# Strassen pairs of a feed-forward layer: another order of the weight splits, row sums spread over three columns, and 13 state units moved into the pairs

## Chip, cores and metric

The kernel runs on one core of one Trainium2 chip. The metric is the device time of one execution in microseconds (us). The kernel before takes 1158.74 us (median of 3 runs, 1157.66 to 1161.28).

## What is computed

One layer of a decoder: 512 prompt tokens and 8 sample tokens (520 columns), width 1024. A modulated norm, one input projection, a pooling branch and a state-space branch, a gated merge and an output projection make up the first 700 us; the change touches none of that. What it touches is the feed-forward block and one small state update:

```python
gt, up = jnp.split(h2 @ w_ffn_in, 2, axis=-1)      # 1024 -> 2 x 2816
x = x + g2 * ((jax.nn.silu(gt) * up) @ w_ffn_out)  # 2816 -> 1024
# sample tokens, one step of the recurrent state: h = h * decay + (dt x) B
```

Everything is float32. A matmul of float32 precision is made of three matmuls on split operands: `hi` is the operand rounded to the PE's format (a copy on ScalarE), `lo` the rest (a subtraction on VectorE), and the product is hi·hi + hi·lo + lo·hi.

## The kernel before

**Columns.** The 2816 hidden channels are 22 columns of 128. A plain column j (`ffn`) multiplies two weight tiles, gate `wg` and up `wu` (128 x 1024 each, 512 KB), with the activations `hh`/`hl` (8 k-tiles of 128 x 520): 8 k-steps for each, 3 matmuls, 2 halves of 260 tokens. Then `ffn_end` applies SiLU on ScalarE and the product on VectorE, into the row `as[j]`.

**Pairs.** Columns 3 to 19 without 8 and 14 (`WINO`, 15 of them) compute gate and up together by one level of Strassen's scheme in Winograd's form (`wino`): seven products of half size instead of eight, 7 x 12 = 84 matmuls of 260 columns. They are called pairs below, since gate and up go together. The scheme needs sums of the activation blocks (`tt`, made once by `sums_of_rows`, `row_cuts` and `more_row_cuts` in rows `as[10]` to `as[17]`) and sums of the weight blocks of each pair. Weights of pair j+1 are prepared while PE multiplies pair j:

- `wino_first(j+1)`: splits one block of u into wx (`wxeh`, `wxel`), starts two sums on POOL (lines 1514 and 1515), then applies SiLU (ScalarE, 1573) and the product (VectorE, 1572) left over from pair j-1, splits the whole gate tile into wg (`wghi`, `wglo`) and starts two more sums on POOL (1523 and 1524), which overwrite parts of it.
- `wino_second(j+1)`: splits the result into wz (`wzhi`, `wzlo`).
- `wino_third(j)`: splits the sums in u into wy (`wyuh`, `wyul`); these two have one buffer each, so that they are made in pair j itself, after the PE has read the ones of pair j-1.

PE's order in a pair is the products g (two), x, z, y, z, y, 12 matmuls each; results are drained by ScalarE (1560) and VectorE (1557), the last of them the addition of the second y product to f2.

**Order.** From `ffn_act` on the program order of PE, ScalarE, VectorE, POOL and the SP queue is the order in which the program states them: each engine works through its own list and waits at the first instruction that is not ready. All weight loads go through SP, and so do the loads of the states; the stores of the states go through POOL's queue.

**Loads.** `pair_load(j+2)` in pair j loads two 512 KB tiles. There are three buffers `raw`; the u tile of an odd pair has a buffer `ur` of its own. Near the plain columns 8 and 14 the next plain column's first tile (wg14, wg20) is loaded early and holds one of the three buffers until it is split.

**Output.** After columns 20 and 21, `ffn_out` makes 8 output columns of 22 k-steps (weights `wfo`, three tiles a column); the last two go together in `last_pair`.

**State units.** `sample_states` handles 32 units of the sample state. A unit loads 256 KB of state `h` and 128 KB of `bb` (a row copied to all partitions), multiplies h by the decay on POOL (1352), makes dt x B with four ScalarE instructions (1358), adds on VectorE (1359) and stores 256 KB from POOL's queue (1360). Unit n asks for the loads of unit n+2. Before, all 32 run inside output columns 0 to 5: five in each of columns 0 to 3, six in columns 4 and 5 (`STEPS`).

Of the kernel before, what the change touches and what calls it, by code (L numbers as in the profile page):

```python
# [16 lines left out]
P = 128  # L17
T = 520
TP = 512
# [24 lines left out]
WARM = 17  # L44
NFS = 3
NU = 40
WINO = [j for j in range(3, 20) if j not in (8, 14)]
STEPS = (4, 8, 12, 16, 20), (3, 6, 10, 13, 17, 20)

SLICES = ((0, 1), (1, 3), (3, 5), (5, 7), (7, 8))  # L50
U_SH1, U_SC1, U_G1, U_SH2, U_SC2, U_G2 = (8 * i for i in range(6))
# [3 lines left out]
def tile_decoder(ctx: ExitStack, tc: tile.TileContext, I: dict, O: dict):  # L55
# [23 lines left out]
    def opened(name, side=None):  # L79
        pool = tc.tile_pool(name=name, bufs=1, **({"side": side} if side else {}))  # L80
        return pool, pool.__enter__()
# [54 lines left out]
    def whole(ps):  # L136
        return [(ps[:, :, :H2], 0, T)]
# [1185 lines left out]
        G["al"] = []  # L1323

    states = {}

    def state_unit(n):

# [2 lines left out]
    def state_load(n):  # L1331
        if n >= 32:
            return
        g, b = state_unit(n)
        sp = G["hs"]
        h = sp.tile([P, 2, 2, P], F32, tag="hs", name=f"hs{n}", bufs=4)
        bb = sp.tile([P, 2, P], F32, tag="bb", name=f"bb{n}", bufs=3)
        nc.sync.dma_start(out=h, in_=I["sssm"][g, :, b : b + 2])
        nc.sync.dma_start(out=bb, in_=dbc[g, 0, b : b + 2].unsqueeze(0).broadcast_to([P, 2, P]))
        states[n] = h, bb  # L1340

    def sample_states():


        for n in range(2):
            state_load(n)
        for n in range(32):
            g, b = state_unit(n)
            state_load(n + 2)
            h, bb = states.pop(n)  # L1350
            at = dtx[:, 1, 2 * g : 2 * g + 2, b : b + 2].rearrange("p j b -> p b j")
            nc.gpsimd.tensor_tensor(h, h, at.unsqueeze(3).broadcast_to([P, 2, 2, P]), ALU.mult)  # L1352
            t = G["ff"].tile([P, T], F32, tag="fs", name=f"ht{n}", bufs=NFS)[:, 0:TP]
            t = t.rearrange("p (b j n) -> p b j n", b=2, j=2)
            for i in range(2):
                for j in range(2):
                    x = xds[:, 2 * g + j, b + i : b + i + 1]
                    nc.scalar.activation(t[:, i, j], bb[:, i], AF.Identity, bias=0.0, scale=x)  # L1358
            nc.vector.tensor_tensor(h, h, t, ALU.add)  # L1359
            nc.gpsimd.dma_start(out=O["ssms"][g, :, b : b + 2], in_=h)  # L1360
            yield True
# [36 lines left out]
    def out_rows_open():  # L1398
        left()
        closed(G["we_"])  # L1400
        closed(G["tt_"])
        G["hx_"], hx = opened("hx")
        G["ah"] = [hx.tile([P, T], F32R, name=f"ah{k}") for k in range(NF)]
        G["hs_"], G["hs"] = opened("hs")

    def out_row(k):

# [28 lines left out]
    def ffn(j):  # L1436
        def fn(wg, wu):
            xh, xl = (lambda k: G["hh"][:, k]), (lambda k: G["hl"][:, k])
            left()
            pg = column([wg], xh, xl)  # L1440
            if j + 1 in WINO:
                wino_first(j + 1)
                pair_load(j + 2)
            pu = column([wu], xh, xl)
            if j + 1 in WINO:
                wino_second(j + 1)
            ffn_end(j, whole(pg), whole(pu))

        return fn
# [12 lines left out]
            t = G["as"][10 + 4 * q + i].rearrange("p (k c) -> p k c", c=H2)  # L1462
            split(*(x[:, 2 * q : 2 * q + 2] for x in G["tt"][i]), t)

    def sums_of_rows():
        v, p = nc.vector.tensor_tensor, nc.gpsimd.tensor_tensor
        add, minus = ALU.add, ALU.subtract
        for q in range(2):
            ks = slice(2 * q, 2 * q + 2)
            b = [[[hblock(n, r, c)[:, ks].bitcast(F32) for c in range(2)] for r in range(2)] for n in ("hh", "hl")]  # L1470
            t1, t2, t3, t4 = (G["as"][10 + 4 * q + i].rearrange("p (k c) -> p k c", c=H2) for i in range(4))
            v(t1, b[0][0][1], b[0][0][0], minus)
            v(t1, t1, b[1][0][1], add)
            v(t1, t1, b[1][0][0], minus)
            v(t2, b[0][1][1], t1, minus)
            v(t2, t2, b[1][1][1], add)
            p(t4, b[0][1][0], t2, minus)
            p(t4, t4, b[1][1][0], add)
            p(t3, b[0][1][1], b[0][0][1], minus)
            p(t3, t3, b[1][1][1], add)  # L1480
            p(t3, t3, b[1][0][1], minus)
        for q in range(2):
            row_cuts(q, 0, 1)

    def more_row_cuts():
        for q in range(2):
            row_cuts(q, 3, 2)

    WW = {}

# [14 lines left out]
    def wino_first(n, mult=None, silu=None):  # L1505


        if n in WINO:
            g, u = WW["raw", n]
            a11, a12, a21, a22 = g[:, 0:4], g[:, 4:8], u[:, 0:4], u[:, 4:8]  # L1510
            WW["x", n] = [G["we"].tile([P, 4, P], F32R, tag=t, name=f"wx{t}{n}", bufs=2) for t in ("eh", "el")]
            split(*WW["x", n], a22)
            v = nc.gpsimd.tensor_tensor
            v(a22, a21, a22, ALU.add)
            v(a21, a11, a21, ALU.subtract)
        elif n <= WINO[-1]:
            ahead(len(W["made"]) + 1)
        if silu:
            silu()
            mult()  # L1520
        if n in WINO:
            split(*wide(n, "g"), g)
            v(a11, a22, a11, ALU.subtract)  # L1523
            v(a12, a12, a11, ALU.subtract)  # L1524

    def wino_second(n):

        if n in WINO:
            split(*wide(n, "z"), WW["raw", n][0])
        else:  # L1530
            ahead(len(W["made"]) + 1, 1)
# [6 lines left out]
    def wino(j):  # L1538
        def fn():
            f1, f2 = (G["ff"].tile([P, T], F32, tag="fs", name=f"fs{j}_{i}", bufs=NFS) for i in range(2))  # L1540
            u2, u4 = f1[:, 0:H2], f2[:, H2:T]
            s = G["as"][j]
            sa, sb = s[:, 0:H2], s[:, H2:T]
            tt = G["tt"]
            B = lambda r, c: (hblock("hh", r, c), hblock("hl", r, c))
            twice = lambda ap: ap.unsqueeze(1).broadcast_to([P, 2, H2])

            def mult(kind, half, x, o=None):
                hi, lo = WW[kind, j]
                o = bank()[:, 0:H2] if o is None else o  # L1550
                for k in range(4):
                    q = 4 * half + k
                    for a, b, f, e in ((hi, x[0], k == 0, False), (hi, x[1], False, False), (lo, x[0], False, k == 3)):
                        nc.tensor.matmul(o, a[:, q], b[:, k], start=f, stop=e)  # L1554
                return o

            add = lambda out, a, b: nc.vector.tensor_tensor(out, a, b, ALU.add)
            m = main()
            wino_first(j + 1, *G.pop("left", ()))
            nc.scalar.copy(u2, mult("g", 0, B(0, 0)))  # L1560
            add(sa, mult("g", 1, B(1, 0)), u2)
            wino_third(j)
            pair_load(j + 2)
            mult("x", 0, tt[3], m[:, 0, 0:H2])
            add(u2, mult("z", 0, tt[1]), u2)
            mult("y", 1, tt[0], m[:, 1, 0:H2])
            wino_second(j + 1)
            add(halves(f2), m[:, :, 0:H2], twice(u2))
            add(sb, mult("z", 1, B(1, 1)), u4)
            add(halves(f2), twice(mult("y", 0, tt[2])), halves(f2))  # L1570
            G["left"] = (
                lambda: nc.vector.tensor_tensor(s, f2, s, ALU.mult),
                lambda: nc.scalar.activation(s, s, AF.Silu, bias=0.0, scale=1.0),
            )
            for kind in "gxyz":
                WW.pop((kind, j))

        return fn
# [17 lines left out]
        return fn  # L1596

    W0, W1 = WINO[0], WINO[-1] + 1
    todo(sums_of_rows)
    for j in range(1, W1):  # L1600
        if j == W0 - 1:
            todo(lambda: (more_row_cuts(), W.update(look=0, loads=0), pair_load(W0)) and None)
        if j in WINO:
            todo(wino(j))
        else:
            todo(ffn(j), I["wfi"][j], I["wfi"][NF + j])
        if j < W0:
            todo(ada_step)
# [15 lines left out]
    def ffn_out(j):  # L1624
        def fn(*ws):
            def hook(kk):
                if kk in (8, 16):
                    ahead(len(W["made"]) + 1, 2)
                if kk in STEPS[j >= 4]:
                    states_step()  # L1630

            ps = column(ws, ah, al, hook)
            x = G["x1"][:, j]
            for s in range(2):
                gate_add(x, ps[:, s, :H2], s * H2, mod[:, U_G2 + j])
            add_square(G["fo"], G["acc"], x, 0, T, j == 0)
            nc.scalar.activation(x, x, AF.Identity, bias=0.0, scale=V["fnw"][:, j : j + 1])

        return fn
# [176 lines left out]
```

## Time and profile before

| | |
|---|---|
| median of 3 runs | 1158.74 us |
| profiled execution | 1160.08 us, of which the span (first to last instruction) is 1158.0 |
| mean granted PE clock | 0.969 |
| PE, DVE, ACT, POOL busy | 93%, 67%, 46%, 29% |
| first plain column to the last pair | 721.1 to 971.1 us |
| plain columns 20 and 21 | 971.1 to 994.2 us |
| output columns | 994.2 to 1146.3 us |

PE is TensorE, DVE VectorE, ACT ScalarE, POOL GpSimd, SP the queue of SyncE. A row of the order in time gives the start and the duration in us, engine, line, operation, output and input tiles and their shape, and in brackets the idle time before it with what ended it. `wglo<-raw,wghi` writes wglo from raw and wghi. A row of the table of stretches gives the stretch, its length, and for each engine its busy time and its count of instructions; then the granted clock, the share of the DMA engines and GB/s. A row of the waits gives who waited for whom, us in total, how often, and the longest.

### The profile page before, as it was taken

To read this page: it belongs to the slowest core of one execution; us is meant where nothing else is said; L and a number is where in the kernel's file an instruction comes from. 1 tells how busy PE (TensorE), PEld (TensorE's weight loads), DVE (VectorE), ACT (ScalarE), POOL (GpSimd) and SP (SyncE) were. 2 spreads that over 40 slices of the span, in tenths; PEclk is the share of its full clock that TensorE was granted. 3 is DMA by queue.
4 is the path that set the end of the run, shared out by engine and by line. 5 is a ranking of instruction groups with operands and counts; after the bars stand their busy time and mean duration, and the time that the engine had idled before them with its cause. 6 is when DMAs were issued, how large, how long until landed. Compare 5 with 4: busy or idle time off the path is not lost.

```text
span 1158.0 us, 22443 instructions
## 1 busy us (share of the span) xinstructions
PE 1079.3 (93%) x9151; PEld 1044.9 (90%) x9151; DVE 780.0 (67%) x1118; ACT 532.8 (46%) x955; POOL 338.8 (29%) x440
## 2 busy tenths in 40 slices
PE   7988999999999999999999998789988879998976
PEld 6987999999999999999999997788888779998876
DVE  5687787777786987886676555867466566554442
ACT  4448556566465436654333335234233336454540
POOL 1133333343334420000000003755443550244421
PEclk8998999999999999999999999899999999998988
DMA  9534563563453324544444542122322123577742
GB/s 362 200 89 145 136 185 91 157 179 110 140 183 116 120 97 164 166 148 151 139 150 144 182 166 99 66 74 73 110 73 110 55 74 96 185 252 247 236 169 74
DMA packets 63590, 165.36 MB, mean 143 GB/s; under 512 B 10880, under 2 KB 20608, under 8 KB 62720
## 3 DMA queue, kind: packets, MB, share of 16 engines
q1 hardware_dynamic: 60928, 155.54, 41.7%
q0 software_dynamic: 2560, 8.39, 1.8%
q8 instruction: 72, 1.18, 0.4%
q14 instruction: 30, 0.25, 0.1%
HBM read 151.05 MB, written 12.86 MB: 142 GB/s over the span
## 4 chain that ended last, share of the span: by engine, by line
PE 54%; DMA 13%; DVE 9%; POOL 9%; ACT 8%; issue 6%; SPq 0%; POOLq 0%; ACTq 0%; DVEq 0%
PE m L131 41%; DMA bb<-dbc 3%; PE b L131 3%; DMA raw<-in_wfi 3%; DMA araw<-in_wada 3%; PE b L1554 2%; POOL raw L1523 2%; PE b L797 2%; POOL raw L1524 1%; DMA out_ssms<-hs 1%; DVE wglo L159 1%; ACT ht L1358 1%; PE b L772 1%; PE b L799 1%; DVE ar L288 1%
## 5 line engine op out<-in xcount | busy, mean ns | idle before, releaser
L131 PE MATMUL m<-hh,whi 128*128 128x260 f32 (+2 forms) x1360 | 285.1, 289 | 7.6 <-ACT v L646 3.6
L131 PE MATMUL m<-hh,wlo 128*128 128x260 f32 (+2 forms) x1360 | 279.0, 285 | 5.3 <-DVE wlo L119 5.2
L131 PE MATMUL m<-hl,whi 128*128 128x260 f32 (+2 forms) x1360 | 278.9, 285 | 0.6 <-DVE hl L483 0.4
L131 PEld LDWEIGHTS m<-hh,whi 128*128 128x128 f32 x1360 | 212.7, 190 | 13.9 <-ACT v L646 3.8
L131 PEld LDWEIGHTS m<-hh,wlo 128*128 128x128 f32 x1360 | 213.1, 190 | 5.8 <-DVE wlo L119 5.8
L131 PEld LDWEIGHTS m<-hl,whi 128*128 128x128 f32 x1360 | 212.7, 190 | 1.2 <-DVE hl L483 0.8
L119 DVE TENSOR_TENSOR wlo<-raw,whi 128x1024 fp32r<-128x1024 f32 (+2 forms) x136 | 166.9, 1232 | 52.4 <-ACT whi L118 51.9
L118 ACT CAST whi<-raw 128x1024 fp32r<-128x1024 f32 (+2 forms) x136 | 138.0, 1020 | 118.4 <-PE m L131 91.2
L654 DVE SCALAR_TENSOR_TENSOR v<-xb,cwh,v 128x512 f32<-128x512 f32 x96 | 72.1, 752 | 39.2 <-POOL xb L641 19.2
L343 POOL TENSOR_TENSOR r<-me,mhalf 128x5 f32<-128x5 f32 (+2 forms) x6 | 6.4, 1066 | 277.8 <-DVE me L342 277.8
L131 PE MATMUL m<-ah,whi 128*128 128x260 f32 x264 | 54.9, 290 | 6.1 <-ACT whi L118 6.1
L1358 ACT ACTIVATE ht<-bb,xds 128x128 f32<-128x128 f32 x128 | 40.7, 391 | 43.1 <-DMA bb<-dbc 42.9
L1359 DVE TENSOR_TENSOR hs<-hs,ht 128x512 f32<-128x512 f32 x32 | 22.2, 693 | 56.4 <-ACT ht L1358 34.9
L158 ACT CAST wzhi<-raw 128x1024 fp32r<-128x1024 f32 x15 | 15.7, 1048 | 89.7 <-POOL raw L1524 89.7
L131 PE MATMUL m<-ah,wlo 128*128 128x260 f32 x264 | 54.9, 290 | 0.8 <-DVE wlo L119 0.8
L645 ACT COPY xb<-m 128x520 f32<-128x520 f32 (+1 forms) x31 | 17.9, 578 | 81.3 <-PE m L131 81.3
L159 DVE TENSOR_TENSOR wzlo<-raw,wzhi 128x1024 fp32r<-128x1024 f32 x15 | 18.4, 1226 | 54.4 <-ACT wzhi L158 54.4
L131 PE MATMUL m<-al,whi 128*128 128x260 f32 x264 | 54.2, 287 | 0.0
L131 PE MATMUL m<-gh,whi 128*128 128x260 f32 x256 | 52.8, 288 | 0.0
L131 PE MATMUL m<-gl,whi 128*128 128x260 f32 x256 | 51.3, 282 | 0.0
L131 PE MATMUL m<-gh,wlo 128*128 128x260 f32 x256 | 51.3, 282 | 0.0
L1352 POOL TENSOR_TENSOR hs<-hs,dtx 128x512 f32<-128x512 f32 x32 | 36.8, 1148 | 46.8 <-DMA hs<-in_sssm 46.2
(385 smaller groups left out, 2679.2 us busy)
## 6 DMA issues: line engine op xcount, KB each, us to landing
raw<-in_win SPq DMA_DIRECT2D x73, 512.0 KB, 5.1
raw<-in_wfi SPq DMA_DIRECT2D x35, 512.0 KB, 3.6
araw<-in_wada SPq DMA_DIRECT2D x24, 512.0 KB, 4.0
h<-in_sssm SPq DMA_DIRECT2D x16, 512.0 KB, 4.3
raw<-in_wssd SPq DMA_DIRECT2D x16, 512.0 KB, 3.6
raw<-in_wfo SPq DMA_DIRECT2D x16, 512.0 KB, 6.2
hs<-in_sssm SPq DMA_DIRECT2D x32, 256.0 KB, 5.5
out_ssms<-hs POOLq DMA_DIRECT2D x32, 256.0 KB, 4.7
```

The source lines that it names most:

```text
L118: nc.scalar.copy(hi, raw)
L119: nc.vector.tensor_tensor(lo, raw, hi.bitcast(F32), ALU.subtract)
L131: nc.tensor.matmul(o, a[:, k, c0 : c0 + P], b[:, t0:t1], start=f, stop=e)
L159: nc.vector.tensor_tensor(lo, src, hi.bitcast(F32), ALU.subtract)
L645: nc.scalar.copy(shape(xb[:, 3 + t0 : 3 + t1]), o)
L654: nc.vector.scalar_tensor_tensor(v[:, 0:TP], xb[:, k : k + TP], w(k), v[:, 0:TP], ALU.mult, ALU.add)
L797: nc.tensor.matmul(o, xdt[:, c, 2 * i + h], dec[:, c, 2 * i + h], start=c == 0, stop=False)
L1352: nc.gpsimd.tensor_tensor(h, h, at.unsqueeze(3).broadcast_to([P, 2, 2, P]), ALU.mult)
L1358: nc.scalar.activation(t[:, i, j], bb[:, i], AF.Identity, bias=0.0, scale=x)
L1359: nc.vector.tensor_tensor(h, h, t, ALU.add)
L1523: v(a11, a22, a11, ALU.subtract)
L1554: nc.tensor.matmul(o, a[:, q], b[:, k], start=f, stop=e)
```

## The change

The change has these parts.

- `WINO` begins at 4: column 3 becomes a plain column, and 14 pairs are left.
- `sums_of_rows` takes a step number: before plain columns 1, 2 and 3 it makes one half of the sums, the other half with two cuts, and the other six cuts (a cut is the split of a sum into hi and lo).
- In a pair, `wino_third(j)` comes first; `wino_first(j+1)` applies the leftover SiLU and product at its end; `wino_second(j+1)` comes after two more drains.
- 13 state units run in columns 4 to 16, one in each. A unit is cut into two steps: decay and dt x B; addition and store. Their tiles lie in the rows `as[17]` to `as[21]`, which hold no results before column 17. There are three rows for h and three half rows for bb.
- The loads of the other 19 units begin in `out_rows_open`; they run in the output columns, four in column 0 and three in columns 1 to 5.

```diff
-WINO = [j for j in range(3, 20) if j not in (8, 14)]
-STEPS = (4, 8, 12, 16, 20), (3, 6, 10, 13, 17, 20)
+WINO = [j for j in range(4, 20) if j not in (8, 14)]
+STATES = 17
...
+    NEARLY = STATES - WINO[0]
...
+        if n < NEARLY:
+            h = G["as"][19 + n % 3][:, 0:TP].rearrange("p (b j n) -> p b j n", b=2, j=2)
+            bb = G["as"][17 + n % 3 // 2][:, n % 3 % 2 * 256 :][:, 0:256].rearrange("p (b n) -> p b n", b=2)
+        else:
...
             state_load(n)
+        yield True
         for n in range(32):
             g, b = state_unit(n)
-            state_load(n + 2)
+            if n >= NEARLY or n + 2 < NEARLY:
+                state_load(n + 2)
...
                     nc.scalar.activation(t[:, i, j], bb[:, i], AF.Identity, bias=0.0, scale=x)
+            yield True
             nc.vector.tensor_tensor(h, h, t, ALU.add)
             nc.gpsimd.dma_start(out=O["ssms"][g, :, b : b + 2], in_=h)
             yield True
...  # out_rows_open
+        for n in range(2):
+            state_load(NEARLY + n)
...  # ffn: one step after wino_first(j + 1), one after wino_second(j + 1)
+                if WINO[0] < j < STATES:
+                    states_step()
...
+    def sums_of_rows(step):
+        if step < 2:
+            row_sums(step)
+        if step:
+            row_cuts(step - 1, 0, 1)
+        if step == 2:
+            row_cuts(0, 3, 2)
+            row_cuts(1, 3, 2)
...  # wino_first
-        if silu:
-            silu()
-            mult()
         if n in WINO:
             split(*wide(n, "g"), g)
             v(a11, a22, a11, ALU.subtract)
             v(a12, a12, a11, ALU.subtract)
+        if silu:
+            silu()
+            mult()
...  # wino
             m = main()
+            wino_third(j)
             wino_first(j + 1, *G.pop("left", ()))
             nc.scalar.copy(u2, mult("g", 0, B(0, 0)))
             add(sa, mult("g", 1, B(1, 0)), u2)
-            wino_third(j)
+            if j < STATES:
+                states_step()
             pair_load(j + 2)
             mult("x", 0, tt[3], m[:, 0, 0:H2])
             add(u2, mult("z", 0, tt[1]), u2)
             mult("y", 1, tt[0], m[:, 1, 0:H2])
-            wino_second(j + 1)
             add(halves(f2), m[:, :, 0:H2], twice(u2))
             add(sb, mult("z", 1, B(1, 1)), u4)
+            wino_second(j + 1)
             add(halves(f2), twice(mult("y", 0, tt[2])), halves(f2))
+            if j < STATES:
+                states_step()
...  # ffn_out
-                if kk in STEPS[j >= 4]:
+                if kk in (3, 6, 10, 13, 17, 20) or (j < 1 and kk in (8, 12)):
                     states_step()
```

More of the change, by code (lines that the diff above doesn't have):

```diff
@@ L1334, in state_load @@
         g, b = state_unit(n)
-        sp = G["hs"]
-        h = sp.tile([P, 2, 2, P], F32, tag="hs", name=f"hs{n}", bufs=4)
-        bb = sp.tile([P, 2, P], F32, tag="bb", name=f"bb{n}", bufs=3)
+        if n < NEARLY:
+            h = G["as"][19 + n % 3][:, 0:TP].rearrange("p (b j n) -> p b j n", b=2, j=2)
+            bb = G["as"][17 + n % 3 // 2][:, n % 3 % 2 * 256 :][:, 0:256].rearrange("p (b n) -> p b n", b=2)
+        else:
+            sp = G["hs"]
+            h = sp.tile([P, 2, 2, P], F32, tag="hs", name=f"hs{n}", bufs=4)
+            bb = sp.tile([P, 2, P], F32, tag="bb", name=f"bb{n}", bufs=3)
         nc.sync.dma_start(out=h, in_=I["sssm"][g, :, b : b + 2])
@@ L1446, in fn @@
                 wino_second(j + 1)
+                if WINO[0] < j < STATES:
+                    states_step()
             ffn_end(j, whole(pg), whole(pu))
@@ L1463, in row_cuts, with row_sums @@
             split(*(x[:, 2 * q : 2 * q + 2] for x in G["tt"][i]), t)
-    def sums_of_rows():
+    def row_sums(q):
         v, p = nc.vector.tensor_tensor, nc.gpsimd.tensor_tensor
         add, minus = ALU.add, ALU.subtract
[L1468 to L1487, printed above, removed]
+        ks = slice(2 * q, 2 * q + 2)
+        b = [[[hblock(n, r, c)[:, ks].bitcast(F32) for c in range(2)] for r in range(2)] for n in ("hh", "hl")]
+        t1, t2, t3, t4 = (G["as"][10 + 4 * q + i].rearrange("p (k c) -> p k c", c=H2) for i in range(4))
+        v(t1, b[0][0][1], b[0][0][0], minus)
+        v(t1, t1, b[1][0][1], add)
+        v(t1, t1, b[1][0][0], minus)
+        v(t2, b[0][1][1], t1, minus)
+        v(t2, t2, b[1][1][1], add)
+        p(t4, b[0][1][0], t2, minus)
+        p(t4, t4, b[1][1][0], add)
+        p(t3, b[0][1][1], b[0][0][1], minus)
+        p(t3, t3, b[1][1][1], add)
+        p(t3, t3, b[1][0][1], minus)
+    def sums_of_rows(step):
[6 more added lines that the diff above has]
+            row_cuts(1, 3, 2)
     WW = {}
@@ L1566, in fn @@
             mult("y", 1, tt[0], m[:, 1, 0:H2])
-            wino_second(j + 1)
             add(halves(f2), m[:, :, 0:H2], twice(u2))
             add(sb, mult("z", 1, B(1, 1)), u4)
+            wino_second(j + 1)
             add(halves(f2), twice(mult("y", 0, tt[2])), halves(f2))
+            if j < STATES:
+                states_step()
             G["left"] = (
@@ L1598, in tile_decoder @@
     W0, W1 = WINO[0], WINO[-1] + 1
-    todo(sums_of_rows)
     for j in range(1, W1):
+        if j < W0:
+            todo(lambda step=j - 1: sums_of_rows(step))
         if j == W0 - 1:
-            todo(lambda: (more_row_cuts(), W.update(look=0, loads=0), pair_load(W0)) and None)
+            todo(lambda: (W.update(look=0, loads=0), pair_load(W0), states_step()) and None)
         if j in WINO:
```

## The prediction

> **What bounds the kernel now.** I read first the busy time in stretches cut at the stage borders, then who TensorE (PE) waited for, then the order of the work inside one pair. The stretches run from the first plain feed-forward column to the start of pair 4, then pairs 4 to 7, plain 8 with pairs 9 to 13, plain 14 with pairs 15 to 19, plain 20 and 21, output columns 0 to 5, and the last two output columns. Columns: length, busy time of PE, PEld, DVE, ACT, POOL, granted clock, DMA share, GB/s.
>
> ```profile
> 721.10:765.75 44.65, 35.56 (x279) 34.90 (x280) 34.06 (x36) 13.26 (x20) 30.03 (x18) 0.92 0.24 82
> 765.75:814.70 48.95, 43.06 (x340) 42.23 (x339) 35.69 (x42) 18.66 (x26) 21.79 (x12) 0.97 0.25 89
> 814.70:892.60 77.90, 66.63 (x517) 65.29 (x516) 46.40 (x53) 24.75 (x34) 32.95 (x20) 0.96 0.24 87
> 892.60:971.10 78.50, 67.00 (x518) 65.54 (x518) 45.30 (x52) 24.59 (x33) 32.93 (x20) 0.96 0.22 75
> 971.10:994.20 23.10, 23.10 (x195) 23.10 (x194) 19.89 (x28) 16.17 (x27) 0.00 (x0) 1.00 0.30 93
> 994.20:1102.10 107.90, 99.98 (x794) 98.68 (x792) 50.05 (x71) 57.03 (x140) 48.05 (x55) 0.95 0.76 243
> 1102.10:1146.30 44.20, 39.08 (x278) 37.85 (x278) 16.31 (x31) 12.58 (x27) 9.64 (x12) 0.88 0.37 124
> ...
> 961.01 0.28 PE L1554 MATMUL b<-hh,wghi 128*128 128x260 f32 x1
> 971.10 0.40 PE L131 MATMUL m<-hh,whi 128*128 128x260 f32 x2
> ```
>
> ```profile
> PE m L1554 <- DVE wyul L159: 26.8, 12, 3.1
> PE m L131 <- DVE wlo L119: 6.0, 3, 5.2
> ```
>
> Plain 20 and 21 have no idle time: 23.10/32 k-steps is 0.722 us a step, so a plain column is 11.55 and an output column (22 steps) 15.9. Pair 19 ran from 961.01 to 971.10: 10.1 without a stall. Against these floors the seven stretches lose 11.5 (two plain columns, one pair), 8.6, 15.8, 16.4, 0, 12.5 and 12.4 us. PE's wait on wyul, 12 times 2.2 us, is the visible end of a cycle over three other engines:
>
> ```profile
> 791.38 1.22 DVE L159 TENSOR_TENSOR wzlo<-raw,wzhi 128x1024 fp32r<-128x1024 f32 x1 [3.28 <-ACT wzhi L158]
> 794.47 0.68 DVE L159 TENSOR_TENSOR wxel<-ur,wxeh 128x512 fp32r<-128x512 f32 x1
> 795.67 2.33 DVE L159 TENSOR_TENSOR wglo<-raw,wghi 128x1024 fp32r<-128x1024 f32 x1
> 798.27 1.95 DVE L159 TENSOR_TENSOR wyul<-raw,wyuh 128x1024 fp32r<-128x1024 f32 x1
> 803.85 1.23 DVE L159 TENSOR_TENSOR wzlo<-raw,wzhi 128x1024 fp32r<-128x1024 f32 x1 [3.29 <-ACT wzhi L158]
> ...
> 795.23 1.70 POOL L1514 TENSOR_TENSOR ur<-ur 128x512 f32<-128x512 f32 x1 [4.96 <-DVE wxel L159]
> 802.76 1.05 ACT L158 CAST wzhi<-raw 128x1024 fp32r<-128x1024 f32 x1 [6.19 <-POOL raw L1524]
> 816.94 2.21 POOL L1514 TENSOR_TENSOR ur<-ur 128x512 f32<-128x512 f32 x1 [14.21 <-DVE wxel L159]
> 823.29 1.05 ACT L158 CAST wzhi<-raw 128x1024 fp32r<-128x1024 f32 x1 [6.82 <-POOL raw L1524]
> ```
>
> From one wzlo to the next: two drains and f2's last addition, wxel, four POOL sums, wzhi, wzlo: 12.47 us, above PE's 10.1. The sums take 7.53 (795.23 to 802.76) with wglo and wyul beside them, 6.35 (816.94 to 823.29) with wglo alone: each two-input DVE operation beside them adds its own length. wyul starts only behind wglo, 6.9 us after wzlo, and PE runs its y products that late.
>
> **The parts and their cost.** *A, row sums over three columns; pair 3 becomes plain.* Now all sums and cuts stand ahead of column 2's two wlo, which run from 739.63 to 744.2:
>
> ```profile
> 739.63 4.53 DVE L119 TENSOR_TENSOR wlo<-raw,whi 128x1024 fp32r<-128x1024 f32 x2
> ```
>
> With one half of the sums a step, wlo of column 2 starts at about 725.4 behind five sums and at 2.3 each is done by 730, before PE wants it at 732.7. The second half starts at 733.5 and its two cuts and wlo of column 3 end near 743 to 745.5, wanted at 744.5. The six cuts left end near 750, so that wxel and the POOL chain of pair 4 give its wzlo near 758 (start). Three unstalled columns and two short adaLN steps on PE: pair 4 starts at 756.2, not 765.75, though pair 3's 10.1 has become 11.55. I take 9.5; bounds 4 (a stall of 5 stays) and 11.
>
> *B, the new order in a pair (4 to 7).* wyul goes first. Its buffer is free when the y products of the pair before end, and its two operations (1.05 and 1.2) lie under PE's next 48 products (5.8 us), so that the buffer costs nothing. After wzlo's start DVE has f2's last addition at 1.1, a state addition at 1.75, wyul at 2.4 and wxel at 3.5; the drains and f2's first addition move under the POOL sums. POOL starts 0.76 later (as 794.47 to 795.23), takes 6.35 and 0.6 for the SiLU product, which now stands beside them, then 1.09 to wzlo: 12.3. So the cycle gains only 0.2, but PE has y at 3.6 after wzlo and ends its pair at 7.7 after it, some 5 us earlier. That phase is gained once per group, before a plain column. Pair 4's wzlo starts at 758.1, then 769.2 (no leftover work), 781.5, 793.8; pair 7 ends at 801.5. It is 45.3 instead of 48.95: 3.6.
>
> *C and D, pairs 9 to 13 and 15 to 19.* wg14 and wg20 hold one of three raw buffers, and a load waits for wzlo:
>
> ```profile
> 824.37 1.23 DVE L159 TENSOR_TENSOR wzlo<-raw,wzhi 128x1024 fp32r<-128x1024 f32 x1 [6.38 <-ACT wzhi L158]
> 829.08 0.62 ACT L158 CAST wxeh<-raw 128x512 fp32r<-128x512 f32 x1 [4.24 <-DMA raw<-in_wfi]
> 838.77 1.23 DVE L159 TENSOR_TENSOR wzlo<-raw,wzhi 128x1024 fp32r<-128x1024 f32 x1 [3.29 <-ACT wzhi L158]
> 843.72 1.05 ACT L158 CAST wghi<-raw 128x1024 fp32r<-128x1024 f32 x1 [1.91 <-DMA raw<-in_wfi]
> 851.51 1.23 DVE L159 TENSOR_TENSOR wzlo<-raw,wzhi 128x1024 fp32r<-128x1024 f32 x1 [1.91 <-ACT wzhi L158]
> 866.32 1.23 DVE L159 TENSOR_TENSOR wzlo<-raw,wzhi 128x1024 fp32r<-128x1024 f32 x1 [3.28 <-ACT wzhi L158]
> ```
>
> This stays. Steps of 14.4, 12.74 and 14.81 become 13.6 (4.71 to wxeh, 1.5 to POOL, 6.35, 1.09), 12.4 and 14.3, as wyul no longer delays the sums. With 9.9 from the plain column to the first wzlo and 7.7 after the last: 9.9+13.6+12.4+14.3+12.4+7.7 = 70.3, not 77.9; in the second group, with states in pairs 15 and 16 only, 69.5, not 78.5. That is 16.6; I leave 2 for slow clock after the stalls that stay: 14.6. Bounds for B to D: 0, if the chain does not shorten, and 33, if PE's floor is reached (8.6+15.8+16.4 less some 8).
>
> *The 13 units in the pairs.* Each adds these four operations, two loads on SP and a store on POOL's queue:
>
> ```profile
> L1352 POOL TENSOR_TENSOR hs<-hs,dtx x32: 1040/1062/1478, 999.4 to 1113.0; 128x512 f32<-128x512 f32 x32
> L1358 ACT ACTIVATE ht<-bb,xds x128: 384/388/406, 1000.3 to 1113.8; 128x128 f32<-128x128 f32 x128
> L1359 DVE TENSOR_TENSOR hs<-hs,ht x32: 691/693/696, 1001.7 to 1114.3; 128x512 f32<-128x512 f32 x32
> L1360 POOL DMA_DIRECT2D out_ssms<-hs x32: 580/580/774, 1002.7 to 1115.3; - x32
> ...
> raw<-in_wfi SPq DMA_DIRECT2D x35, 512.0 KB, 3.6
> out_ssms<-hs POOLq DMA_DIRECT2D x32, 256.0 KB, 4.7
> bb<-dbc SPq DMA_DIRECT2D x32, 128.0 KB, 5.8
> ```
>
> POOL's 1.06 falls in its gap behind the fourth sum (4.96 before the next), ACT's four (1.55) in its 6.19 before wzhi, the DVE addition is in the cycle above, and the store's 0.58 ends before wxel. On SP the load of unit n+2 into one of three rows waits for the store of unit n-1: issued some 3 after wzlo, landed 4.7 later, so that pair j+2's loads behind it go out at about 8.5 after wzlo and land at 12 to 13; wxel wants them at 15.8 (12.3+3.5). Free with 3 us to spare; without that cover up to 3 a pair. In C and D the late half of the loads waits for wzlo anyway.
>
> The Trainium skill, "SBUF — State Buffer", section "Who interferes with whom", has the shared DVE and POOL port as a lock held for a whole instruction, also by two-input DVE operations against POOL reads; the 7.53 against 6.35 agrees.
>
> *E, the output stage with 19 units instead of 32.* Three per column, four in the first, not five and six.
>
> ```profile
> ACT ht L1358 <- DMA bb<-dbc: 42.9, 19, 5.7
> 1026.00:1042.00 16.00, 16.00 (x135) 16.00 (x135) 8.89 (x13) 8.06 (x21) 7.29 (x9) 1.00 0.83 250
> 1102.12 0.39 PE L131 MATMUL b<-ah,whi 128*128 128x256 f32 x1 [1.10 <-ACT whi L118]
> ```
>
> ACT waits for bb, the casts of the next weights stand behind it, and the last two columns begin without them. A unit moves 640 KB and a column 1408 KB, so that five units need 297 GB/s where 250 were moved; three need 214. The first columns, at 250, did not stall. Of 24.9 lost I take 22 back; bounds 10 and 25.
>
> Sum: 9.5+3.6+14.6+22 = 49.7, from the profiled execution's 1160.08 (its span of 1158.0 and 2.1 around it) to 1110.4. The median of the runs, 1158.74, is 1.3 below it: 1109.
>
> **The rivals.**
> 1. The pair cycle does not shorten (port and loads hold the sums as long): A and E alone, 1158.7-31.5 = 1127. For it: the cycle's sum is 12.3 against 12.47. Against: wyul's place.
> 2. The output stage gives half (loads of the last two columns stay late): 1109+11 = 1120. Against: SP's queue then has 40% fewer state loads.
> 3. PE's floor is reached in the pairs: 33 for B to D, 1109-15 = 1094. Against: the loads of C and D.
> 4. The other side: ACT's state operations wait for bb in the pairs as they did outside, and wzhi stands behind them. At the longest wait seen, 5.7, times 13 units, beyond ACT's gap, 74 us against 49.7: 1158.7+24 = 1183. It decides from 3.8 us a unit on. Against: bb is asked for two pairs ahead, some 17 us before use, and the median landing is 5.8.
> 5. DVE holds up the store's issue on POOL. Were it held until wyul, wxel, wglo and the SiLU product are through, its 0.58 would end at 6.5 after wzlo, and the sums, which the same operations delay anyway, would end 0.5 later: 6 us in the eleven pairs with states, 1115. Against: L1360's 580/580/774 among busy DVE work. The same page's box on the DVE and DMAs from the POOL queue has 620 ns become 3100 beside a DVE copy in a two-port mode; with 3.1 for the 0.58 the sums would start 1.3 later, 14 us, and the sum be 1123. The trace shows no such issue.
>
> **How the numbers follow.** Forecast 0.56 (1109, its own range 1101 to 1118); rivals in order 0.13, 0.13, 0.06, 0.05 and 0.04; nothing measurable 0.03. No change is within 0.3%, some 3.5 us. Faster is the forecast and rivals 1, 2, 3 and 5 (0.92), slower rival 4; the range 1098 to 1132 leaves out rivals 3 and 4 and some of the rest.
>
> **What would show it.** A: no wait on wlo near 740. B: PE's waits on wyul under 1.2 us, new ones on wzlo of 1 to 3, wzlo to wzlo 12.3. C and D: wxeh and wghi still released by DMA. E: bb waits under 10 us in all, output columns near 15.9, the last two near 33. Wrong, if POOL's first sum waits for a store, ACT in the pairs for bb, or SP's weight loads land after wxel wants them.

## The result and the profile after

The changed kernel takes 1112.14 us (median of 4 runs, 1110.73 to 1116.53), the kernel before 1158.2 beside it (median of 4); the ratio is 0.9608, interval 0.9571 to 0.9646. The forecast was 1109.0, range 1098 to 1132. The profiled execution of the changed kernel is the longest of its four, 1116.53, with a span of 1114.7.

First the table of stretches of the changed kernel, cut at the same borders as before (plain columns 1 to 3, where the kernel before had 1, 2 and pair 3; pairs 4 to 7; 8 to 13; 14 to 19; plain 20 and 21; output 0 to 5; the last two). Columns: stretch, length, busy time of PE, PEld, DVE, ACT, POOL, granted clock, DMA share, GB/s.

```profile
723.98:758.88 34.90, 34.90 (x290) 34.90 (x291) 26.14 (x32) 10.81 (x16) 22.41 (x13) 1.00 0.35 114
758.88:804.31 45.43, 41.99 (x339) 40.77 (x337) 32.04 (x40) 22.26 (x40) 26.35 (x20) 1.00 0.40 131
804.31:877.74 73.43, 66.65 (x519) 64.19 (x518) 49.31 (x60) 31.49 (x57) 38.97 (x32) 0.98 0.42 141
877.74:951.12 73.38, 66.49 (x518) 64.21 (x517) 45.99 (x59) 28.60 (x46) 34.70 (x27) 0.98 0.35 115
951.12:974.74 23.62, 23.34 (x194) 23.14 (x193) 21.75 (x29) 16.06 (x27) 1.05 (x1) 1.00 0.34 117
974.74:1069.90 95.16, 95.16 (x794) 95.16 (x793) 48.06 (x66) 47.88 (x107) 29.58 (x36) 1.00 0.69 218
1069.90:1102.90 33.00, 33.00 (x278) 33.00 (x277) 10.25 (x24) 5.61 (x9) 2.74 (x4) 1.00 0.20 66
```

In the first and the last two stretches PE is busy for the whole length, at clock 1.00: nothing is lost there any more. The seven differ from before by 9.75, 3.5, 4.5, 5.1, -0.5, 12.7 and 11.2 us, 46.3 in all. The first stretch begins 2.9 later than before (723.98, not 721.10), in a part that the change does not touch; 46.3 less 2.9 is the difference of the spans, 43.3, within rounding.

Whom PE waited for from 690 us on (total, times, longest), the rows that replace wyul's 26.8 and wlo's 6.0:

```profile
PE b L1570 <- DVE as L1573: 5.8, 6, 1.8
PE m L1570 <- DVE wyul L159: 5.0, 8, 0.6
PE b L1570 <- ACT fs L1577: 3.0, 4, 1.2
PE b L1570 <- DVE wzlo L159: 3.0, 4, 0.8
...
PE m L131 <- DVE wlo L119: 0.3, 1, 0.3
```

No wait is large any more. The first row is new. Its longest case, on VectorE and on PE, in pair 11:

```profile
850.14 2.23 DVE L159 TENSOR_TENSOR wglo<-raw,wghi 128x1024 fp32r<-128x1024 f32 x1 [0.26 <-ACT wghi L158]
852.29 1.76 DVE L1592 TENSOR_TENSOR as<-fs,as 128x520 f32<-128x520 f32 x1
853.98 0.42 DVE L1573 TENSOR_TENSOR as<-b,fs 128x260 f32<-128x260 f32 x1
```

```profile
854.45 0.39 PE L1570 MATMUL b<-hh,wghi 128*128 128x260 f32 x1 [1.79 <-DVE as L1573]
```

The drain at 853.98 stands behind wglo and the SiLU product, which take 2.23 and 1.76 beside POOL's sums, where operations of these lengths without them take 1.22 and 0.69; PE's g product goes on when that drain has read its result out.

VectorE's order in one undisturbed pair, and POOL's beside it:

```profile
784.45 1.23 DVE L159 TENSOR_TENSOR wzlo<-raw,wzhi 128x1024 fp32r<-128x1024 f32 x1 [2.81 <-ACT wzhi L158]
785.59 0.69 DVE L1573 TENSOR_TENSOR fs<-b,fs 128x520 f32<-128x520 f32 x1
786.20 0.68 DVE L1367 TENSOR_TENSOR as<-as,ht 128x512 f32<-128x512 f32 x1
786.80 1.22 DVE L159 TENSOR_TENSOR wyul<-raw,wyuh 128x1024 fp32r<-128x1024 f32 x1
787.94 0.68 DVE L159 TENSOR_TENSOR wxel<-ur,wxeh 128x512 fp32r<-128x512 f32 x1
...
796.48 1.22 DVE L159 TENSOR_TENSOR wzlo<-raw,wzhi 128x1024 fp32r<-128x1024 f32 x1 [2.81 <-ACT wzhi L158]
```

```profile
788.71 2.19 POOL L1530 TENSOR_TENSOR ur<-ur 128x512 f32<-128x512 f32 x1 [0.93 <-DVE wxel L159]
...
794.08 1.29 POOL L1537 TENSOR_TENSOR raw<-raw 128x512 f32<-128x512 f32 x1
795.33 1.05 POOL L1359 TENSOR_TENSOR as<-as,dtx 128x512 f32<-128x512 f32 x1
```

From wzlo to wzlo 12.03: 3.49 to wxel, 0.77 to POOL, four sums in 6.66 (788.71 to 795.37), 1.11 to the next wzlo. wyul is now 2.35 behind wzlo, not 6.9. The state multiply stands behind the fourth sum, in a gap.

### The profile page after: what moved, and what is told of

It reads as the page before. It is cut to its first block, busy times and chain, and to the rows that moved or that the text cites. A ratio compares the mean times of both kernels' runs of the same rounds, so it can differ in the third digit from the quotient of the medians.

```text
span 1114.7 us, 22415 instructions
## 1 busy us (share of the span) xinstructions
PE 1068.8 (96%) x9163; PEld 1034.6 (93%) x9163; DVE 767.9 (69%) x1111; ACT 528.1 (47%) x952; POOL 319.8 (29%) x436
## 4 chain that ended last, share of the span: by engine, by line
PE 67%; DMA 8%; POOL 8%; DVE 6%; ACT 5%; issue 4%; SPq 1%; POOLq 0%; ACTq 0%; DVEq 0%
PE m L131 54%; PE b L131 4%; DMA raw<-in_wfi 2%; DMA raw<-in_win 2%; POOL raw L1536 2%; PE b L1570 1%; PE b L797 1%; POOL raw L1537 1%; DMA araw<-in_wada 1%; DMA ur<-in_wfi 1%; DMA araw<-in_wad 1%; PE b L772 1%; PE b L799 1%; ACT wzhi L158 1%; PE b L209 1%
## 5 line engine op out<-in xcount | busy, mean ns | idle before, releaser
L131 PE MATMUL m<-hh,whi 128*128 128x260 f32 (+2 forms) x1392 | 292.0, 289 | 3.6 <-ACT v L646 3.5
L131 PE MATMUL m<-hh,wlo 128*128 128x260 f32 (+2 forms) x1392 | 285.2, 285 | 0.4 <-DVE wlo L119 0.3
L131 PE MATMUL m<-hl,whi 128*128 128x260 f32 (+2 forms) x1392 | 285.0, 284 | 0.3 <-DVE hl L483 0.2
L119 DVE TENSOR_TENSOR wlo<-raw,whi 128x1024 fp32r<-128x1024 f32 (+1 forms) x138 | 175.5, 1276 | 79.9 <-ACT whi L118 77.1
L131 PEld LDWEIGHTS m<-hh,whi 128*128 128x128 f32 x1392 | 218.1, 190 | 9.6 <-ACT v L646 3.7
L131 PEld LDWEIGHTS m<-hl,whi 128*128 128x128 f32 x1392 | 217.8, 190 | 0.7 <-DVE hl L483 0.4
L118 ACT CAST whi<-raw 128x1024 fp32r<-128x1024 f32 (+1 forms) x138 | 140.4, 1022 | 155.8 <-PE m L131 125.5
L818 POOL TENSOR_TENSOR h<-h,cc 128x1024 f32<-128x1024 f32 x16 | 39.0, 2437 | 27.9 <-DMA cc<-dbc 27.0
L288 DVE TENSOR_TENSOR ar<-araw,aw 128x1024 f32<-128x1024 f32 x24 | 29.4, 1224 | 18.6 <-ACT aw L287 18.4
L131 PEld LDWEIGHTS m<-gh,whi 128*128 128x128 f32 x256 | 39.2, 188 | 2.4 <-PE b L303 1.1
## 6 DMA issues: line engine op xcount, KB each, us to landing
araw<-in_wad SPq DMA_DIRECT2D x6, 1024.0 KB, 14.6
```

The costliest lines, as they stand in the source:

```text
L118: nc.scalar.copy(hi, raw)
L119: nc.vector.tensor_tensor(lo, raw, hi.bitcast(F32), ALU.subtract)
L131: nc.tensor.matmul(o, a[:, k, c0 : c0 + P], b[:, t0:t1], start=f, stop=e)
L288: nc.vector.tensor_tensor(r, raws[n], w1, ALU.subtract)
L818: nc.gpsimd.tensor_tensor(h0, h0, cc.unsqueeze(2).broadcast_to([P, 4, 2, P]), ALU.mult)
```

## The experiments

Medians and ratios to the kernel before, which ran beside them (1158.8 to 1159.1):

| | kernel | us | ratio (interval) |
|---|---|---|---|
| 1 | row sums spread, old order in a pair, 32 units in the output | 1148.21 | 0.9917 (0.9892 to 0.9942) |
| 2 | row sums and new order, 32 units in the output | 1124.42 | 0.9707 (0.9684 to 0.9730) |
| 3 | row sums and 13 units in the pairs, old order | 1132.08 | 0.9776 (0.9752 to 0.9801) |
| 4 | the change, weight loads asked for ahead of state loads | 1111.46 | 0.9600 (0.9572 to 0.9629) |
| 5 | the change, wg14 and wg20 not loaded early | 1103.92 | 0.9525 (0.9498 to 0.9552) |
| 6 | 4 and 5 together | 1100.78 | 0.9495 (0.9470 to 0.9520) |
| 7 | the change without the 13 units | 1103.42 | 0.9516 (0.9490 to 0.9542) |
| 8 | before, ScalarE reads one bb that stays | 1152.33 | 0.9944 (0.9920 to 0.9968) |
| 9 | 6, state addition and store one pair later | 1102.97 | 0.9518 (0.9492 to 0.9544) |
| 10 | the change, more DMA bytes in the output | 1113.21 | 0.9599 (0.9566 to 0.9632) |
| 11 | before, no loads of bb | 1150.07 | 0.9929 (0.9902 to 0.9956) |
| 12 | 11 with five rows of h, loads three ahead | 1151.67 | 0.9930 (0.9903 to 0.9956) |

### 1 to 3: the three parts alone

Experiment 1 undoes the order in the pair and the units; 2 only the units; 3 only the order. In 1 and 2 `STATES` is 0, and a unit is one step again, as before:

```diff
# units back (1, 2)                      # order back (1, 3)
-    NEARLY = STATES - WINO[0]           -            wino_third(j)
+    NEARLY = 0                                       wino_first(j + 1, ...)
...                                      ...
-if kk in (3, 6, 10, 13, 17, 20) or ...  +            wino_third(j)
+if kk in STEPS[j >= 4]:                 ...          # wino_second, silu likewise
```

> Only the row sums spread over columns 1 to 3, with column 3 plain; the pairs in their old order, all 32 units in the output columns. Theory (each stage gives back its own stall, the stages add): the 8 us wait near 740 goes, 9.7 us as in the trace of the changed kernel, 1148.5. Rival (the moved state units carry the whole gain; sums and pair order only shift a wait to the next one): 1158, within 3 of the kernel before.

> Sums spread and new order in the pairs, all 32 units in the output columns. Theory: beside the 9.7 of the sums the pairs give 13 as measured with states, and some 10 more, since 11 state additions of 0.6 leave the cycle and no state load stands ahead of a weight load: 1125; wzlo to wzlo 11.4 in pairs 5 to 7; the output stage keeps its 25 us loss. Rival 1 (the cycle is held by the POOL sums, the order gives nothing): 1148. Rival 2 (the moved units carry all): 1158.

> Sums spread and 13 units in the pairs, the pairs in their old order. Theory: 9.7 and 24 are given back, and the units cost 0.6 in each of 11 cycles and some 4 by SP's queue, since the old order has no slack for them: 1135. Rival (the moved units carry all the gain, the order none): 1112 to 1115, as the changed kernel.

The sums bring 10 (1158.2 to 1148.2), as the theory had it. The order brings 24 on top of them (1148.2 to 1124.4), or 20 with the units in place (1132.1 to 1112.1). The units bring 16 with the old order and 12 with the new. The rival for 3, under which the order is worth nothing, falls; PE's wait on wyul stays in full there:

```profile
PE m L1570 <- DVE wyul L159: 24.3, 13, 2.8
```

The output of 2, with all 32 units in it and the new order ahead of it, in the table of stretches:

```profile
960.25:1063.52 103.27, 97.91 (x794) 96.84 (x793) 51.25 (x72) 57.71 (x143) 48.39 (x57) 0.98 0.79 255
1063.52:1108.81 45.29, 38.38 (x280) 37.52 (x278) 15.06 (x29) 11.87 (x26) 8.47 (x11) 0.89 0.35 118
```

It takes 148.6; with 19 units it takes 128.2. So 20.4 is the gain of the units there (fewer of them, and cut in two), yet the whole time falls by 12.3 only. Something of 8 is paid in the pairs.

### 7: the price of the units in the pairs

The 13 units are not computed at all, so that this part of the output state is missing:

```diff
-        for n in range(2):
-            state_load(n)
         yield True
         for n in range(32):
+            if n < NEARLY:
+                yield True
+                yield True
+                continue
```

> The changed kernel with the 13 units of the pairs left out altogether (their states are not computed; 19 remain in the output columns): the price of the units in the pairs. Theory: 0.6 in each of 11 cycles and some 4 by SP's queue at pairs 9 and 15: 1102, with wzlo to wzlo 11.4. Rival (the units lie in idle time of every engine and cost nothing): 1112.

1103.42 against 1112.14: 8.7 us, which nearly closes the account of 2 (20.4 less 8.7 is 11.7, measured 12.3). A step is the time from the start of one pair's wzlo to that of the next. In the trace the way from pair 4's wzlo to pair 19's is 171.9 without the units and 182.6 with them (761.32 to 943.89). Where the 10.7 lie, from the wzlo starts on VectorE:

```profile
781.89 1.23 DVE L159 TENSOR_TENSOR wzlo<-raw,wzhi 128x1024 fp32r<-128x1024 f32 x1 [2.79 <-ACT wzhi L158]
793.33 1.23 DVE L159 TENSOR_TENSOR wzlo<-raw,wzhi 128x1024 fp32r<-128x1024 f32 x1 [2.82 <-ACT wzhi L158]
810.86 1.23 DVE L159 TENSOR_TENSOR wzlo<-raw,wzhi 128x1024 fp32r<-128x1024 f32 x1 [5.01 <-ACT wzhi L158]
```

An ordinary step is 11.44 without a unit and 12.03 with one: the state addition's 0.6, no more. But across plain column 8, 17.53 without units became 21.31 (796.48 to 817.79), and across column 14, 17.53 became 21.81: 8.1 of the 10.7. The trace of the changed kernel shows why. SP's queue (start and length of an issue), ScalarE, VectorE and POOL around plain column 8, which PE starts at 804.31:

```profile
801.80 0.33 SPq L1343 DMA_DIRECT2D as<-in_sssm  x1
802.22 0.57 SPq L1344 DMA_DIRECT2D as<-dbc  x1
802.90 0.37 SPq L1512 DMA_DIRECT2D ur<-in_wfi  x1
```

```profile
808.97 0.62 ACT L158 CAST wxeh<-ur 128x512 fp32r<-128x512 f32 x1 [3.44 <-DMA ur<-in_wfi]
```

```profile
798.24 0.68 DVE L1367 TENSOR_TENSOR as<-as,ht 128x512 f32<-128x512 f32 x1
...
799.97 2.07 DVE L119 TENSOR_TENSOR wlo<-raw,whi 128x1024 fp32r<-128x1024 f32 x1
...
806.52 0.68 DVE L1367 TENSOR_TENSOR as<-as,ht 128x512 f32<-128x512 f32 x1
...
809.63 0.69 DVE L159 TENSOR_TENSOR wxel<-ur,wxeh 128x512 fp32r<-128x512 f32 x1 [1.81 <-ACT wxeh L158]
```

```profile
799.82 1.14 POOL L1359 TENSOR_TENSOR as<-as,dtx 128x512 f32<-128x512 f32 x1
```

The load of ur for pair 9 stands behind the state's two loads, which wait for the store of an older unit. It leaves at 802.90 and has landed at 808.97; VectorE stands for 1.81 until wxeh is made. Two state additions ahead of wxel, those of pairs 6 and 7, take 0.6 each, and a wlo of the plain column takes 2.07 instead of 1.22 beside POOL's state multiply. 1.81 + 1.2 + 0.85 = 3.9, of a measured 3.8. So about half is the late load, and half is VectorE's own work.

### 4, 5 and 6: the two loads

In 4 the weight loads go ahead of the state loads in a step, in 5 the early load of the next plain column's gate tile is dropped, in 6 both:

```diff
+            pair_load(j + 2)              # 4 and 6, in pairs and plain columns
             if j < STATES:
                 states_step()
-            pair_load(j + 2)
...
-            ahead(len(W["made"]) + 1, 1)  # 5 and 6
+            ahead(len(W["made"]) + 1)
```

> The changed kernel with the weight loads of pair j+2 asked for ahead of the state loads in each pair and in columns 8 and 14. Theory: SP stands at a state load until the store of unit n-1 has landed, and the loads of pair 9 and 15 behind it come some 2 us late for wxel and wghi; with them first, wzlo of pair 9 and 15 comes 1.8 earlier each, 1108.5, and the wait of wxeh on ur near 807 and 880 goes. Rival (the plain column's own work on VectorE is what delays wxel): 1112, no change.

> The changed kernel without the early load of wg14 and wg20: these tiles are asked for two columns ahead like the others, so that all three raw buffers serve the pairs. Theory: the steps of some 13.9 from wzlo of an odd pair to that of the next even one (four in the profile) wait for a load that waits for wzlo; with a third buffer they fall to 12.0 to 12.3, 1105. Rival (the load is late for SP's queue or the DMA engines, not for a buffer): steps stay near 13.9, 1112.

> The kernel of the late plain loads and the weight loads asked for ahead of the state loads. Weight loads first gave 1.9 and 2.3 back at pairs 9 and 15 and lost 0.3 to 0.6 in each later step of two buffers, as the state loads then left together with the weight load that the cycle waits for. Theory: with three buffers that load no longer waits for wzlo, so the 4 remain: 1101 to 1103. Rival (state loads and weight loads collide in any order): as the one with late plain loads alone, 1105.

4 missed: 1111.46 against 1112.14, no measurable difference where the runs of either kernel spread over some 6 us. The step it was made for came as expected: across column 8 it is 19.44 instead of 21.31, across column 14 19.47 instead of 21.81, and the wait on ur is gone. Of these 4.2, 1.7 are lost again in the pairs that follow, 14.07 and 14.19 instead of 13.76 and 13.87 behind column 8; from pair 4's wzlo to pair 19's the traces still differ by 2.5 (182.57 and 180.03). wzlo on VectorE and SP's queue in experiment 4 (x3 is three issues, taken together):

```profile
816.24 1.23 DVE L159 TENSOR_TENSOR wzlo<-raw,wzhi 128x1024 fp32r<-128x1024 f32 x1 [6.37 <-ACT wzhi L158]
830.31 1.23 DVE L159 TENSOR_TENSOR wzlo<-raw,wzhi 128x1024 fp32r<-128x1024 f32 x1 [2.80 <-ACT wzhi L158]
```

```profile
803.75 14.07 SPq L109 DMA_DIRECT2D raw<-in_wfi  x3
817.92 0.38 SPq L1343 DMA_DIRECT2D as<-in_sssm  x1
```

The weight load that waits for a buffer (to 817.8) now holds the state loads behind it, and they leave with it, at the moment when the pair wants that tile. That this is what lengthens those steps is read from the rows; no run has it alone. In 5 the third buffer is free, no load of the pairs behind column 8 waits for wzlo, and the steps after it fall to 11.7 and 12.0 at once:

```profile
817.81 1.23 DVE L159 TENSOR_TENSOR wzlo<-raw,wzhi 128x1024 fp32r<-128x1024 f32 x1 [4.99 <-ACT wzhi L158]
829.50 1.23 DVE L159 TENSOR_TENSOR wzlo<-raw,wzhi 128x1024 fp32r<-128x1024 f32 x1 [3.95 <-ACT wzhi L158]
841.54 1.23 DVE L159 TENSOR_TENSOR wzlo<-raw,wzhi 128x1024 fp32r<-128x1024 f32 x1 [2.82 <-ACT wzhi L158]
```

It gains 8.2. With both edits, 6 has 19.44 across each plain column and 11.1 to 12.05 everywhere else, and is the fastest kernel here: 1100.78, 11 us below the change. Against 5 that is 3.1 in the medians and 2.7 in the same stretch of the traces (171.78 and 169.05). So the order of the loads is worth about as much in the traces with the third buffer as without it; alone it is too small for these runs to show.

### 9: the state addition taken out of the cycle

From 6, with the addition and the store of a unit one pair later and ahead of wzlo, where VectorE stands idle for 2.8; the loads, the multiply and dt x B of the next unit move to the same place:

```diff
-            if j < STATES:
-                states_step()
             pair_load(j + 2)
...
+            states_pair(j)        # addition and store of the last unit, decay of this one
             wino_second(j + 1)
```

> The best kernel so far (late plain loads, weight loads first), with the VectorE addition and the store of a unit one pair later and ahead of wzlo, where VectorE waits some 2.8 us for wzhi. Theory: in wzlo to wzlo of 12.04 the state addition of 0.6 stands in the chain; moved into the wait it costs nothing, 11.4 a step in 11 pairs: 1094. Rival (the POOL sums set the step, the addition beside them takes the shared port instead): 12.0 stays, 1101.

1102.97, not 1094: the rival holds. The addition was priced at its own 0.6 in the cycle, but at its new place it costs as much. VectorE, then POOL, in experiment 9:

```profile
789.86 0.96 DVE L1367 TENSOR_TENSOR as<-as,ht 128x512 f32<-128x512 f32 x1
793.08 1.60 DVE L159 TENSOR_TENSOR wzlo<-raw,wzhi 128x1024 fp32r<-128x1024 f32 x1 [2.26 <-ACT wzhi L158]
```

```profile
790.36 1.62 POOL L1541 TENSOR_TENSOR raw<-raw 128x512 f32<-128x512 f32 x1
792.53 1.06 POOL L1359 TENSOR_TENSOR as<-as,dtx 128x512 f32<-128x512 f32 x1
```

The addition lengthens POOL's fourth sum from 1.29 to 1.62, and the state multiply, which now comes right after it, lengthens wzlo from 1.23 to 1.60. The step stays at 12.1.

### 8 and 10 to 12: what holds the output stage

```diff
# 8, 11, 12 (from before): ScalarE's dt x B reads one row for all units
+        stay = G["hs"].tile([P, 2, P], F32, tag="bs", name="bstay", bufs=1)
-            h, bb = states.pop(n)
+            h, bb = states.pop(n)[0], stay        # 8: bb is loaded, into 2 buffers instead of 3, and not read
...
-        nc.sync.dma_start(out=bb, in_=dbc[...])   # 11 and 12: bb is not loaded
...
# 12: bufs=5 for h instead of 4
-            state_load(n + 2)
+            state_load(n + 3)
# 10 (from the change): five copies of 256 KB in each output column
+                if kk in (2, 5, 9, 14, 18):
+                    spare = dp.tile([P, 4, P], F32, name=f"spare{uid()}")
+                    nc.sync.dma_start(out=spare, in_=I["wfi"][2 * j][:, 0:4])
```

> The kernel before, with the four ScalarE operations of every unit reading one bb that was loaded once (states of the other units come out with that bb); all loads and stores stay, with their bytes. Theory: in the output columns ScalarE's wait for bb holds the casts of the next weights behind it; without it 15 or more of the 25 us come back, 1141. Rival (the stage is bound by DMA bandwidth, 297 GB/s wanted and 250 had, so the weights themselves come late): under 5 come back, 1154 or more.

> The changed kernel with five copies of 256 KB a column from memory to memory in the six output columns, as many bytes as the two or three units that were taken out of them, and nothing waits for them (extra work, no result). Theory as forecast (five units ask for 297 GB/s where 250 are moved, so the weights come late): the stage loses 15 or more again, 1127. Rival (the stage before was held by the units' own chain of load, POOL, VectorE, store and by engines that wait in it, not by bandwidth): 1112 to 1116.

> The kernel before without the loads of bb: one bb serves all units (their states come out with it), 255 GB/s wanted instead of 297. Bandwidth: most of the 25 us come back, 1140. The units' chain (a row of h is free again only when its store has landed; four rows, load 5.5, POOL 1.06, VectorE 0.7, issue 0.6 and store 4.7 are 12.6 for four units, and a column of five has 12.7): little more than with the bytes kept, 1150.

> As the run with one bb and no bb loads, with five rows for h instead of four and loads asked for three units ahead: the same bytes, a looser chain. The units' chain: 10 or more come back against four rows, 1138. Bandwidth: within 3 of the run with four rows.

In 10 the rival holds, and the bandwidth of the forecast falls. 8 lies between its two theories. In 11 the theory of bytes falls a second time, and in 12 the theory that put rows of h in its place falls too. The output columns of 10 in the table of stretches:

```profile
971.98:1067.14 95.16, 95.16 (x794) 95.16 (x793) 45.80 (x64) 46.16 (x102) 29.55 (x36) 1.00 0.90 300
```

300 GB/s were moved, as much as the forecast said five units want, and PE was busy for all of the 95.16. So many bytes alone do not hold the stage. Experiment 8's output, in which ScalarE never waits for bb, and 11's, which moves 128 KB a unit less:

```profile
991.26:1094.16 102.90, 97.67 (x795) 97.41 (x793) 49.97 (x73) 59.30 (x151) 48.76 (x57) 0.97 0.82 265
1094.16:1137.82 43.66, 36.21 (x280) 35.51 (x278) 14.78 (x29) 8.57 (x17) 7.62 (x10) 0.92 0.32 104
```

```profile
997.76:1098.51 100.75, 97.56 (x795) 96.73 (x794) 52.70 (x72) 58.77 (x150) 49.01 (x57) 0.98 0.71 231
1098.51:1139.15 40.64, 35.20 (x279) 34.59 (x278) 14.98 (x29) 8.99 (x19) 7.84 (x11) 0.96 0.33 107
```

Up to the start of the last matmul the kernel before takes 151.8, 8 takes 146.6 and 11 takes 141.4: some 5 and 10 back, of about 24 that the change gives. So the loads of bb are not free (in the medians 11 is 2.3 below 8), but they are not the whole. In place of ScalarE's wait for bb, VectorE waits for POOL's multiply of the same unit, with the next weights' wlo behind the addition in its order (from the waits of 8):

```profile
DVE hs L1361 <- POOL hs L1354: 50.6, 28, 4.1
```

More rows of h (12) change nothing that can be measured (1151.67 against 1150.07). Left open: whether the stage comes free by the smaller number of units in a column, or by the cut of a unit into two steps, after which the addition is stated some k-steps behind the multiply. In all, VectorE's additions stood for ScalarE or POOL for 56.4 us before, 51.5 in 8 and 3.7 in the change. A third candidate is SP's queue, in which the weight loads stand behind state loads that wait for stores: 62.6 us before, 55.4 in 8, 11.0 in the change. No run changed one of the three alone. But the trace of 8 narrows it: the four columns with five units each, and then the second of those with six:

```profile
991.26:1054.86 63.60, 63.60 (x533) 63.60 (x532) 31.02 (x45) 37.41 (x93) 30.28 (x35) 1.00 0.82 263
1070.70:1094.16 23.46, 18.23 (x132) 17.97 (x130) 10.23 (x15) 12.00 (x32) 10.70 (x13) 0.85 0.81 265
```

Five units a column that are not cut cost PE nothing there, once ScalarE does not wait for bb. The first column with six (1054.86 to 1070.70) has no idle time either; the loss begins in the second. Whether six in two columns would pass if they were cut, no run shows.

## Why the prediction was right, and where it was not

- **A, 9.5.** Measured 9.75 in the stretch and 10 in experiment 1.
- **B, 3.6 and a step of 12.3.** 3.5 and 12.03. The sums took 6.66 where the sum had 6.95. PE's waits on wyul are 0.6 at most and 5.0 in all (expected under 1.2), on wzlo 0.8 (expected 1 to 3). Not foreseen was the wait on the drain behind wglo, 5.8 in all.
- **C and D, 16.6 worked out, 14.6 taken; measured 9.6.** This is the term that was mis-sized. The steps inside were near: 13.76, 12.23, 13.87 and 12.25 against 13.6, 12.4, 14.3 and 12.4, and 7.8 for the tail. What failed is the 9.9 from the plain column to the first wzlo: it took 13.5 (804.31 to 817.79) and 14.0 (877.74 to 891.71). Without the units (experiment 7) it is 10.3 at both places (800.55 to 810.86, 869.35 to 879.66), near the 9.9, which thus held nothing for the units. Two things were missing in it. The first is in the sentence "Free with 3 us to spare": it was worked out in an ordinary pair, where POOL's chain gives the loads 12.3 us; around a plain column that cover is missing, and the third sign of being wrong, weight loads that land after wxel wants them, came there. Experiment 4 takes that wait away and gets 1.9 and 2.3 back across the two columns. The second is VectorE: with the loads out of the way (4 and 6) the step is still 19.44, 1.9 above the 17.53 without units, which are the two additions and the longer wlo. The fallback "up to 3 a pair" covers the first only.
- **E, 22.** Measured about 24: the floor of 15.9 a column is reached (95.16/6). The size was right and the cause was not: neither the bandwidth (experiment 10) nor ScalarE's wait for bb (experiment 8, some 5 of 24) carries it. The 22 was taken from the loss against PE's floor, so its being right says nothing for the cause. Nor is the 24 idle time alone: the same 794 matmuls took 99.98 at a granted clock of 0.95 before and 95.16 at 1.00 after, and 278 took 39.08 at 0.88 and 33.00 at 1.00, together 10.9.
- **The sum.** 9.75 + 3.5 + 9.6 + 24 = 46.8 against 49.7: 5 less than taken in C and D, 2 more in E; plain columns 20 and 21 lost 0.5, which gives 46.3. The median missed by 3.1 (1112.14 against 1109). That the errors in C and D and in E partly cancel is luck.
- **The rivals.** 1 falls, since the order is worth 20 to 24; 2, since the output reached its floor; 3, since B to D gave 13.1 of its 33. 4, the slower side: no wait for bb stands among the waits in the pairs, where bb is asked for two pairs ahead. 5: the store's issue on POOL's queue keeps its length among two-input work of VectorE:

```profile
L1368 POOL DMA_DIRECT2D out_ssms<-as x13: 580/586/774, 775.2 to 920.9; - x13
```

The Trainium skill has a DMA from POOL's queue go from about 620 to about 3100 ns beside a copy on VectorE ("SBUF — State Buffer", section "A bandwidth-pool intuition that's wrong (but worth ruling out)"). No issue in this kernel came near that; the VectorE work around them is two-input additions and subtractions.

## What to carry to other kernels

Work that is added to a software pipeline is to be priced at the place where the pipeline's cover is thinnest, here the plain columns between pairs, and not in an ordinary step: the units cost 0.6 us in an ordinary step and about 4 in a step across a plain column. In an in-order load queue every load that waits for a store or a buffer delays what stands behind it; look for who stands behind before you choose the order. Here the buffer was worth more (experiment 5, 8 us) than the order (some 2.5 in the traces, with and without the buffer). A size that comes out right does not prove its cause: put the suspected load back and see whether the loss returns.

## What the runs showed of the hardware

The DMA engines moved 300 GB/s at a share of 0.90 over 95 us with no idle time of PE that the trace shows (95.16 busy of 95.16, experiment 10). Between VectorE and POOL, two-input operations that meet add their times almost in full: in experiment 9 POOL's multiply ends at 793.59 and wzlo beside it at 794.68, 1.09 later. That agrees with the Trainium skill, "SBUF — State Buffer", section "Who interferes with whom", which has the shared port held for a whole instruction. So an idle gap of VectorE was no free place: the addition of 0.6 that was moved there came back as 0.33 on the sum beside it, and as 0.37 on wzlo beside the multiply, which the store's issue ahead of it had pushed there.
